# A first weight tile read in permuted row order, in two transfers, with x copied into the same order

## The chip, the core and the metric

The kernel runs on one core of a Trainium2 chip. The metric is the device time of one launch in microseconds (us). Three runs of the kernel before took 184.22, 182.49 and 182.88 us; the median is 182.88 us. One of them, the one of 184.22 us, was recorded by the hardware profiler, and every duration quoted below is from that execution.

## What is computed

For each of four batch entries the kernel takes a window of 64 consecutive rows of x, which starts at a row given at run time, and multiplies it by one shared matrix w:

```python
B, S, D, W = 4, 4096, 4096, 64
for b in range(B):
    o = int(offsets[b])
    results.append(x[b, o:o+W] @ w)      # x: B x S x D, w: D x D, float32
return np.stack(results)                 # 4 x 64 x 4096, float32
```

Together this is one product of 256 rows with a 4096 x 4096 matrix. w is 64 MiB in float32 and every element of it is read once; the four windows of x are 4 MiB, the output is 4 MiB.

## The kernel before

**Tiling.** The contracted dimension (4096) is cut into 32 k tiles of 128 rows of w. The 256 rows of x are two groups, g = 0 and 1, of 128. A product step is a matmul of a 128 x 128 piece of transposed x with a 128 x 512 piece of w, added up in a PSUM bank (`mm`, line 158).

**Loads of w.** Nearly all of w is loaded by the gpsimd (POOL) queue, which turns float32 into float16 on the way (`load_block`, line 84). The k tiles are loaded in blocks, `blocks` = (first tile, number of tiles): (0, 1), (1, 2), (3, 4), (7, 4), (11, 4), (15, 4), (19, 3), (22, 3), (25, 2), (27, 1). In a block of r tiles, partition p takes r consecutive rows of w, so that one contiguous run of DRAM fills it. `x_cols` picks the columns of x that belong to such an order of rows. Tiles 28 to 31 are loaded in six column pieces (line 122). The blocks go into a ring of three buffers (`wc_pool`, bufs=3): a load is issued only once the work that read the buffer's earlier content is done, and POOL waits for that in program order.

**The first k tile** is different. It is loaded without conversion by the sync (SP) queue, as float32, with one transfer whose pieces are 8 KB (half a row of w; line 67), into the first buffer of the same ring (`w0_32`, line 65). ScalarE (ACT) then converts it to float16 in two halves (line 70) into `w_one`. Row p of w lies on partition p.

**x.** The offsets come by the ACT queue (line 68). POOL loads each offset into a register and issues one transfer per batch entry (line 103), again converting, into `x16` (called `xrow` in the profile). These four transfers stand on the POOL queue behind block (1, 2) and ahead of block (3, 4). Then 64 matmuls with an identity transpose x (line 144), eight to a pair of PSUM banks; VectorE (DVE, line 153) and ACT (line 155) copy the pairs, in turn, to `xT`. All transposes stand ahead of the first product in PE's program order, and both conversions of line 70 stand ahead of line 155 in ACT's.

**Order of the work.** The schedule is written out by hand. `whole_rows(range(0, 3), True)` (line 190) multiplies k tiles 0, 1 and 2 for all columns, and DVE and ACT copy the sums to `acc` (lines 186 and 188). Then `whole_rows` runs once for each block from (3, 4) to (22, 3), and DVE adds the sums to `acc` (line 168). The last blocks and the tail pieces are done by column halves (`columns`, lines 206 to 217, and the loops behind it), and the results are stored from POOL, ACT and SP (line 204).

The three buffers of the ring are given out in this order: first tile, (1, 2), (3, 4), then (7, 4) in the first tile's buffer, (11, 4) in that of (1, 2), (15, 4) in that of (3, 4), and so on.

Of the kernel before, what the change touches and what calls it, by code (L numbers as in the profile page):

```python
# [10 lines left out]
def kernel(  # L11
# [7 lines left out]
    nc = tc.nc  # L19
    fp32 = mybir.dt.float32  # L20
    fp16 = mybir.dt.float16

    B, S, D = x.shape
    _, N = w.shape
    WIN = out.shape[1]
    P = 128
    NT = 512
    NG = N // 2
    n_k = D // P
    n_sub = NG // NT  # L30
    G = B // 2
# [7 lines left out]
    R_MAX = 4  # L39

    const_pool = ctx.enter_context(tc.tile_pool(name="const", bufs=1))
    x_pool = ctx.enter_context(tc.tile_pool(name="xp", bufs=1))
    wc_pool = ctx.enter_context(tc.tile_pool(name="wc", bufs=3))
# [6 lines left out]

    x16 = x_pool.tile([P, G * D], fp16, name="xrow")
    xT = [x_pool.tile([P, D], fp16, name=f"xT{g}") for g in range(G)]
    w_one = w1_pool.tile([P, N], fp16, name="w1")
    tmp = [acc_pool.tile([P, 2 * NT], fp32, name=f"tmp{i}") for i in range(G)]
    acc = [acc_pool.tile([P, N], fp32, name=f"acc{g}") for g in range(G)]
# [5 lines left out]

    ctx.enter_context(tc.manual_schedule())


    w0_32 = wc_pool.tile([P, R_MAX * N], fp16, name="wc", tag="wc")[:].bitcast(fp32)
    w0_32 = w0_32.rearrange("p (h n) -> p h n", h=2)[:, :, :NG]
    nc.sync.dma_start(out=w0_32, in_=w[0:P, :].rearrange("p (h n) -> p h n", h=2))
    nc.scalar.dma_start(out=off_t[:], in_=offsets[None, :])
    for h in range(2):
        nc.scalar.copy(out=w_one[:, h * NG : (h + 1) * NG], in_=w0_32[:, h, :])  # L70
    off_i32 = off_t.bitcast(mybir.dt.int32)


# [21 lines left out]
    for b in range(B):  # L95
# [8 lines left out]
            out=x16[b * PB : (b + 1) * PB, :],  # L104
            in_=x[b][bass.ds(o, WIN), :].rearrange("(p g) d -> p (g d)", g=G),
# [13 lines left out]
    for ng, st in zip(order, (steps, fine_steps)):  # L119
        for ki, n, c0, c1 in st:  # L120
            wd = c1 - c0
            nc.gpsimd.dma_start(  # L122
                out=t[:, pos : pos + n * wd].rearrange("p (t n) -> p t n", t=n),
                in_=w[ki * P : (ki + n) * P, ng * NG + c0 : ng * NG + c1].rearrange(
                    "(t p) n -> p t n", p=P
                ),
            )
            for q in range(n):
                for j in range(wd // NT):
                    a = pos + q * wd + j * NT  # L130
                    tail[(ki + q, (ng * NG + c0) // NT + j)] = t[:, a : a + NT]
            pos += n * wd

    def x_cols(g, kt):
        for k0, r in blocks:
            if k0 <= kt < k0 + r:
                a = k0 * P + kt - k0
                return x16[:, g * D + a : g * D + a + r * (P - 1) + 1 : r]
        return x16[:, g * D + kt * P : g * D + (kt + 1) * P]

    for g in range(G):
        for t in range(4):
            for i in range(8):
                nc.tensor.matmul(  # L144
                    out=pairs[t][:, i * P : (i + 1) * P],
                    lhsT=x_cols(g, 8 * t + i),
                    rhs=identity[:],
                    start=True,
                    stop=True,
                )  # L150
            dst = xT[g][:, 2 * t * NT : 2 * (t + 1) * NT]
            if t % 2 == 0:
                nc.vector.tensor_copy(out=dst, in_=pairs[t][:])  # L153
            else:
                nc.scalar.copy(out=dst, in_=pairs[t][:])  # L155
# [116 lines left out]
```

## Time and profile before

| | |
|---|---|
| median of three runs | 182.88 us (182.49 to 184.22) |
| the profiled execution: own time | 184.22 us |
| the profiled execution: span from first to last instruction | 182.4 us |
| TensorE (PE) busy | 128.3 us, 70% |
| DVE busy | 82.2 us, 45% |
| ACT busy | 16.8 us, 9% |
| queue q0 (POOL's), share of the 16 DMA engines | 92.2% |
| queue q1 (SP's), share of the 16 DMA engines | 4.6% |
| mean granted clock of TensorE | 0.926 |

The core has 16 DMA engines, and all queues run on them. The page's row "DMA" gives, in tenths, the mean busy share of these 16 in 40 equal slices of the span. A row of a queue gives its packets, their megabytes as written, and the time that they took as a share of 16 engines' span. Besides data a queue carries packets of 4 bytes, by which a DMA engine reports that its part of a transfer is done. In the tables of windows, "x" counts instructions, and the last three columns are PE's granted clock, the DMA share and GB/s.

### The profile page before, as it was taken

Reading aid. Unit: us, or ns where it says so; the run is one execution under the profiler, and the core shown is the slowest. Engines: PE = TensorE matmul, PEld = TensorE weight load, DVE = VectorE, ACT = ScalarE, POOL = GpSimd, SP = SyncE. Lnnn points to the kernel's source line nnn. Section 1 sums busy time; section 2 is a strip of 40 time slices with the busy share of each in tenths; the row PEclk is TensorE's granted clock in tenths of the full one; section 3 lists DMA queues with packets and bytes.
Section 4 is the critical chain, followed back from the end, with each engine's and each line's share of the span. In section 5 each row is a group of like instructions: output and inputs, shape, how many; then the busy total and the mean of one; then the engine's idle time right before and its main releaser. Section 6 shows DMA issues by size and latency. Waiting matters only on the chain.

```text
span 182.4 us, 1399 instructions
## 1 busy us (share of the span) xinstructions
PE 128.3 (70%) x576; PEld 57.5 (32%) x576; DVE 82.2 (45%) x68; ACT 16.8 (9%) x15; POOL 12.6 (7%) x27
## 2 busy tenths in 40 slices
PE   0000006998399929995899569999939999999920
PEld 0000006743134403442344224444403444444400
DVE  0000003845036722576077605779933893606570
ACT  2000802643000000000000000000000003104000
POOL 4400010001000010001000100011080000000200
PEclk9999999999969985999699978999975999999996
DMA  4999999999999799999999799999999999999696
GB/s 126 320 259 269 201 205 230 230 234 223 230 223 208 172 208 230 230 226 223 223 230 208 169 237 210 221 216 216 221 208 219 190 208 215 214 212 194 245 406 275
DMA packets 4007, 40.97 MB, mean 225 GB/s; under 512 B 418, under 2 KB 418, under 8 KB 2210
## 3 DMA queue, kind: packets, MB, share of 16 engines
q0 software_dynamic: 3152, 36.70, 92.2%
q1 hardware_dynamic: 560, 3.15, 4.6%
q10 hardware_dynamic: 290, 1.05, 1.4%
q8 instruction: 4, 0.07, 0.1%
q14 instruction: 1, 0.01, 0.0%
HBM read 71.30 MB, written 4.19 MB: 414 GB/s over the span
## 4 chain that ended last, share of the span: by engine, by line
DMA 62%; PE 26%; issue 4%; DVE 2%; POOLq 1%; DVEq 1%; POOL 1%
DMA wc<-in_w_dram 62%; PE banks L158 26%; DVE acc L168 2%; DVEq L267 1%; POOLq L96 1%; POOL xrow L103 0%; POOL identity masks.py:197 0%; POOLq L103 0%; POOL wc L84 0%; POOLq masks.py:199 0%; DVEq L168 0%; POOLq L256 0%
## 5 line engine op out<-in xcount | busy, mean ns | idle before, releaser
L158 PE MATMUL banks<-wc,xT 128*128 128x512 f16 x496 | 121.9, 405 | 17.2 <-DMA wc<-in_w_dram 17.0
L168 DVE TENSOR_TENSOR acc<-acc,banks 128x1024 f32<-128x1024 f32 x56 | 67.9, 1220 | 59.7 <-PE banks L158 58.7
L158 PEld LDWEIGHTS <-xT 128*128 128x128 f16 x512 | 52.3, 103 | 87.5 <-DMA wc<-in_w_dram 19.4
L144 PE MATMUL banks<-identity,xrow 128*128 128x128 f16 x64 | 5.4, 269 | 28.8 <-DMA xrow<-in_x_dram 28.8
L153 DVE CAST xT<-banks 128x1024 f16<-128x1024 f32 x4 | 4.8, 1222 | 30.5 <-PE banks L144 30.5
L213 ACT COPY tmp<-banks 128x1024 f32<-128x1024 f32 x4 | 3.9, 1016 | 118.5 <-PE banks L158 118.5
L144 PEld LDWEIGHTS <-xrow 128*128 128x128 f16 x64 | 5.3, 130 | 28.8 <-issue 28.8
L84 POOL DMA_DIRECT2D wc<-in_w_dram x9 | 4.9, 546 | 113.4 <-PE banks L158 96.9
L186 DVE COPY acc<-banks 128x1024 f32<-128x1024 f32 x4 | 4.9, 1225 | 4.5 <-PE banks L158 4.5
L158 PE MATMUL banks<-w,xT 128*128 128x512 f16 x16 | 6.1, 379 | 0.0
L70 ACT CAST w<-wc 128x2048 f16<-128x2048 f32 x2 | 3.7, 1894 | 16.3 <-DMA wc<-in_w_dram 16.3
L155 ACT CAST xT<-banks 128x1024 f16<-128x1024 f32 x4 | 3.9, 1014 | 8.7 <-PE banks L144 8.7
L217 DVE TENSOR_TENSOR acc<-acc,tmp 128x1024 f32<-128x1024 f32 x4 | 4.7, 1220 | 0.0
L188 ACT COPY acc<-banks 128x1024 f32<-128x1024 f32 x4 | 4.0, 1012 | 6.4 <-PE banks L158 6.4
L122 POOL DMA_DIRECT2D wc<-in_w_dram x6 | 3.9, 676 | 9.3 <-PE banks L158 9.3
L204 POOL DMA_DIRECT2D out_dram<-acc x2 | 1.1, 537 | 33.3 <-DVE acc L217 33.3
L103 POOL DMA_DIRECT2D xrow<-in_x_dram x4 | 2.0, 500 | 2.2 <-issue 2.2
L70 ACT ACT_TABLE_LOAD x1 | 1.3, 1283 | 1.4 <-PEq L256 1.4
masks.py:199 POOL TENSOR_SCALAR_AFFINE_SELECT identity<-identity 128x128 f16<-128x128 f16 x1 | 0.3, 287 | 0.1
masks.py:197 POOL MEMSET identity<- 128x128 f16 x1 | 0.2, 223 | 0.0
L256 POOL MEMSET const-float32-0.0<- 128x1 f32 x1 | 0.1, 98 | 0.4 <-issue 0.4
L256 POOL MEMSET const-bfloat16-1.0<- 128x1 bf16 x1 | 0.1, 102 | 0.0
(2 smaller groups left out, 0.2 us busy)
## 6 DMA issues: line engine op xcount, KB each, us to landing
wc<-in_w_dram POOLq DMA_DIRECT2D x4, 4096.0 KB, 42.0
wc<-in_w_dram POOLq DMA_DIRECT2D x2, 3072.0 KB, 34.3
wc<-in_w_dram POOLq DMA_DIRECT2D x2, 2048.0 KB, 20.2
wc<-in_w_dram POOLq DMA_DIRECT2D x4, 1024.0 KB, 26.7
wc<-in_w_dram SPq DMA_DIRECT2D x1, 2048.0 KB, 18.1
xrow<-in_x_dram POOLq DMA_DIRECT2D x4, 512.0 KB, 20.2
out_dram<-acc POOLq DMA_DIRECT2D x2, 1024.0 KB, 5.0
out_dram<-acc ACTq DMA_DIRECT2D x2, 512.0 KB, 4.5
```

The costliest lines, as they stand in the source:

```text
L70: nc.scalar.copy(out=w_one[:, h * NG : (h + 1) * NG], in_=w0_32[:, h, :])
L84: nc.gpsimd.dma_start(out=t[:, base : base + r * N], in_=w[k0 * P : (k0 + r) * P, :].rearrange("(p r) n -> p (r n)", r=r),)
L122: nc.gpsimd.dma_start(out=t[:, pos : pos + n * wd].rearrange("p (t n) -> p t n", t=n), in_=w[ki * P : (ki + n) * P, ng * NG + c0 : ng * NG ...
L144: nc.tensor.matmul(out=pairs[t][:, i * P : (i + 1) * P], lhsT=x_cols(g, 8 * t + i), rhs=identity[:], start=True, stop=True,)
L153: nc.vector.tensor_copy(out=dst, in_=pairs[t][:])
L155: nc.scalar.copy(out=dst, in_=pairs[t][:])
L158: nc.tensor.matmul(out=banks(bank), lhsT=xT[g][:, kt * P : (kt + 1) * P], rhs=rhs, start=start, stop=stop,)
L168: nc.vector.tensor_add(out=dst, in0=dst, in1=banks(bank, n))
L186: nc.vector.tensor_copy(out=dst, in_=banks(b0, 2))
L188: nc.scalar.copy(out=dst, in_=banks(b0, 2))
L213: nc.scalar.copy(out=tmp[g][:], in_=banks(4 * g + 2, 2))
L217: nc.vector.tensor_add(out=dst, in0=dst, in1=tmp[g][:])
```

## The change

The first k tile is loaded by two transfers on the sync queue, one for each half of the columns, in place of one. Partition 16 b + a now holds row 8 a + b of the tile, so neighbouring partitions lie 8 rows apart in DRAM; in the transfer's source the outermost dimension counts 8 (b), the next 16 (a), the last the 2048 columns. The tile is read into `acc[1]`, which is not otherwise used so early, in place of a buffer of the `wc` ring. The ring therefore gives its first buffer to block (1, 2), its second to (3, 4), its third to (7, 4), and its first again to (11, 4).

So that the products fit, the 128 columns of x that meet this tile are copied into the same order, into a new tile `x_first`, by two DVE copies (one for each g), ahead of the transposes. The transposes of k tile 0 read `x_first`; all others read `x16` as before.

```diff
+    x_first = x_pool.tile([P, G, P], fp16, name="xfirst")
...
-    w0_32 = wc_pool.tile([P, R_MAX * N], fp16, name="wc", tag="wc")[:].bitcast(fp32)
-    w0_32 = w0_32.rearrange("p (h n) -> p h n", h=2)[:, :, :NG]
-    nc.sync.dma_start(out=w0_32, in_=w[0:P, :].rearrange("p (h n) -> p h n", h=2))
+    w0_32 = acc[1]
+
+    w0_rows = w[0:P, :].rearrange("(a b) n -> b a n", b=8)
+    nc.sync.dma_start(out=w0_32[:, :NG], in_=w0_rows[:, :, :NG])
     nc.scalar.dma_start(out=off_t[:], in_=offsets[None, :])
-    for h in range(2):
-        nc.scalar.copy(out=w_one[:, h * NG : (h + 1) * NG], in_=w0_32[:, h, :])
+    nc.sync.dma_start(out=w0_32[:, NG:], in_=w0_rows[:, :, NG:])
+    nc.scalar.copy(out=w_one[:, :NG], in_=w0_32[:, :NG])
+    nc.scalar.copy(out=w_one[:, NG:], in_=w0_32[:, NG:])
...
     def x_cols(g, kt):
+        if kt == 0:
+            return x_first[:, g, :]
...
+    for g in range(G):
+        nc.vector.tensor_copy(
+            out=x_first[:, g, :].rearrange("p (b a) -> p b a", b=8),
+            in_=x16[:, g * D : g * D + P].rearrange("p (a b) -> p b a", b=8),
+        )
```

## Prediction

> **What bounds the kernel now.** I read the page's row of the DMA engines first, then its list of queues, then PE in order of time.
>
> ```profile
> DMA  4999999999999799999999799999999999999696
> q0 software_dynamic: 3152, 36.70, 92.2%
> q1 hardware_dynamic: 560, 3.15, 4.6%
> q10 hardware_dynamic: 290, 1.05, 1.4%
> ```
>
> The 16 DMA engines are busy from the second slice to the last loads; three queues take 98% of their time. The question for any edit is therefore what it does to the work of a DMA engine. PE shows how they pass it on:
>
> ```profile
> 48.71 15.67 PE L158 MATMUL banks<-wc,xT 128*128 128x512 f16 x64 [3.93 <-DMA wc<-in_w_dram]
> 68.02 16.64 PE L158 MATMUL banks<-wc,xT 128*128 128x512 f16 x64 [3.63 <-DMA wc<-in_w_dram]
> 87.29 15.55 PE L158 MATMUL banks<-wc,xT 128*128 128x512 f16 x64 [2.63 <-DMA wc<-in_w_dram]
> 106.61 26.03 PE L158 MATMUL banks<-wc,xT 128*128 128x512 f16 x112 [3.77 <-DMA wc<-in_w_dram]
> 135.66 4.88 PE L158 MATMUL banks<-wc,xT 128*128 128x512 f16 x11 [3.02 <-DMA wc<-in_w_dram]
> ```
>
> Landings start the blocks, 19.3 us apart for four tiles, and PE needs some 16 us for one. The last wait ends at 135.66; from there PE works almost without a break to 174.4, and the last adds and stores follow. If block (22, 3) and the loads behind it land later by d, the end comes later by d.
>
> In the trace's DMA records a transfer ends with one 4-byte report from each DMA engine that took part. Every load of POOL has 16, close together: those of (22, 3) lie between 133.8 and 135.3 us. A packet of a four-tile block takes 2.43 us, eight per engine make 19.45 us, the step of the landings: each engine runs through its own list without a gap, and a block has landed when the **slowest** engine is through.
>
> **The change part by part.**
>
> *The spread of the first tile.* Before, it is 256 packets of 8 KB; an undisturbed one takes 309 ns. q1's 560 packets are these 256, 256 of the stores and 48 reports: three transfers over 16 engines each. So each engine carried 16 of the tile's packets, 16 x 0.309 = 4.94 us. q10 shows another spread: its 290 are 256 of the stores, 32 reports, and for the offsets one packet with **one** report. A transfer with 128 rows outermost went over 16 engines, one with a single row over one. The new source has 8 outermost, between these rows. Its least cost is 0, if it still uses 16 engines. The other end is one engine, 256 x 0.309 = 79 us; I exclude it, since a single row leaves nothing to share out and eight groups do. I take eight engines, one per group, as an estimate from the two rows. Then each of eight engines carries 32 packets, 9.9 us, and the others none: the heavy eight gain 16 x 0.309 = **4.94 us** of work, and the light eight have none of this tile.
>
> [...]
>
> *What can be won back.* Blocks are dealt out in equal parts, so the light engines can't help, and the heavy ones never run dry: 4.94 us stays with them to the last load. If the engines that report latest (135.1 to 135.3, three of 16) were all among the light ones, the end would move up to 1.5 us less; for three at random that is one chance in ten (8/16 x 7/15 x 6/14), so I take off nothing. On the other side, the 256 packets took 92.8 us as recorded, 363 ns in the mean with slow ones at the start; 16 x 0.363 = 5.8 us, 0.9 more.
>
> *Rows 8 apart.* The pieces stay 8 KB. The nearest rows are the tail loads of 4 KB packets, which read pieces of 8 KB that lie 16 KB apart at 0.324 us each: at most 16 x 0.015 = 0.2 us more, at least 0. I take 0.
>
> *The second issue on SP* takes about 0.63 us, as the first at 0.87, and is over before the first data packet at 2.30 us. Behind it SP only has stores, after a wait of 173.1 us. 0. ACT's issue of the offsets does not move.
>
> *The start: ACT behind the second half.* In order of time, before:
>
> ```profile
> 19.02 3.70 ACT L70 CAST w<-wc 128x2048 f16<-128x2048 f32 x2 [16.33 <-DMA wc<-in_w_dram]
> 23.01 0.53 POOL L84 DMA_DIRECT2D wc<-in_w_dram  x1 [15.64 <-ACT w L70]
> 28.84 5.44 PE L144 MATMUL banks<-identity,xrow 128*128 128x128 f16 x64 [28.84 <-DMA xrow<-in_x_dram]
> 30.75 1.01 ACT L155 CAST xT<-banks 128x1024 f16<-128x1024 f32 x1 [8.03 <-PE banks L144]
> ```
>
> The tile has the engines to itself from 2.3 to 6.0 us; nine packets per engine go through. Then q0's packets alternate with it, one for one: seven more packets, the last beside block (1, 2). On a heavy engine 23 packets are left at 6.0. Block (1, 2) and x are 16 packets of 1.227 us with 16 to 20 of the tile's 0.322 between them: x lands at 6.0 + 19.6 + 5.2 to 6.4, about 31 to 32.5 us on the slowest engine in place of 28.4. The four to nine turns left alternate with packets of 2.43 us, 2.75 us a turn, so the **second half lands between 42 and 56 us**. ACT's conversion of it (1.9 us) stands ahead of all copies of line 155, and without them PE cannot finish the transposes. The first products, at 34.26 before, then start at 47 to 61, and end 10.5 us later at 57 to 71, in place of 44.8. Behind them POOL waits to issue (11, 4), at 45.08 before. But q0 still holds (7, 4): the heavy engines have work until 67.6 + 4.9 = 72.5, the light ones until about 65. PE then runs four-tile blocks in 14 to 16 us against 19.45, and is waiting for loads again after one to three blocks. So this delay of 12 to 26 us costs **0 at the end**, as long as (11, 4) reaches the heavy engines by 72.5; the light ones have some 7 us in hand, the heavy ones' 4.9 and the 7 x 0.322 = 2.3 that they no longer carry behind 6.0.
>
> *Two copies to x_first.* No such DVE row exists; the nearest is line 153, 1.22 us for 1024 columns. An eighth of it is 0.15 us, so a copy costs 0.15 to 1.22; I take 0.2. The first transposes wait for one, and line 153 stands behind both. All of it lies in the same cover, and without it 0.4 us would come on the path.
>
> *The buffer.* POOL's wait of 15.64 us ahead of (7, 4) goes; its issue moves from 23.01 to about 7.4. Its data can't move before (3, 4) is through at 48.3, so this wins 0; the next wait is that for (11, 4), just priced. acc[1]'s first other writers follow products that need both conversions anyway: 0.
>
> *PE's clock.* After the wait at 135.66 the granted clock is 0.50 from 136 to 140 and 0.79 to 144, 5.7 us at half speed, some 2.8 us of work. A shifted wait can meet it otherwise; half of this either way, 1.4 us, is an estimate; I take 0.
>
> The sum is +4.9 us. The profiled execution took 184.22 (span 182.4, 1.8 around it) and would take 189.1, with a span of 187.3. It was the slowest of three, 1.34 above the median; the median becomes 182.88 + 4.9 = **187.8**.
>
> **The rivals.**
>
> *Still 16 engines.* The permuted source is spread like any 128 rows. For it speaks that the destination still has 128 rows; against it, the offsets' single report. Then the load per engine is unchanged, the copies are hidden, and it takes 182.9: not slower.
>
> *The heavy engines run dry.* With the first products ending at 71, the issue of (11, 4), and 1.8 to 4.6 us to its first packet (POOL's first load: issued at 1.38, first packet at 5.99), it comes at up to 75.6, 3.1 us after 72.5: 187.8 + 3.1 = 190.9. It decides once the first products end later than about 68 us. Against it stands that this is the late end of every step.
>
> *Faster.* Sixteen engines, and the last wait shifted so that the clock's 5.7 us at half speed go: 182.9 - 2.8 = 180.1. For it speaks only that the mean clock differs from block to block; against it, that the change moves no landing then.
>
> **How the numbers follow.** Eight engines without a gap 0.83; 16 engines 0.09; heavy engines dry 0.05; faster 0.03. The first case spans 187.8 - 2.0 (late engines and clock, mostly one or the other) to 187.8 + 2.3 (slow packets and clock), 185.8 to 190.1. That holds about 0.95 x 0.83 = 0.79; with a little of the third case 190.4 reaches 0.8. Changes within 1% are about what a measurement of this kernel can't tell from none. Slower by over 1%: 0.83 + 0.05; within 1%: 0.09; faster 0.03.
>
> **What would show it.** q1's packets: 256 + 256 + 32 reports of stores + 2 x 8 = 560 with eight engines, 576 with sixteen. x landing near 32 and the first products ending at 57 to 71, not 45; the reports of a block in two groups some 7 us apart; PE's last wait ending near 140.6. The prediction is wrong if the second group isn't there, if the heavy engines have a gap after 65 us, or if the last PE wait is set by something other than a load.

## The result, and the profile after

The change makes the kernel **20 us slower**: 202.92 us (202.54 to 204.88) against 182.97 us (182.49 to 184.41), six runs each, a ratio of 1.109 (95% interval 1.103 to 1.116). The direction was forecast, the size was not: the prediction was 187.8 us, its range ended at 190.4. The profiled execution has a span of 201.0 us, 18.6 more than the one before.

The page's row of the DMA engines and its queues, of the kernel after:

```profile
DMA  4999999999999859999999998999999999985697
q0 software_dynamic: 3152, 36.70, 87.3%
q1 hardware_dynamic: 560, 3.15, 6.9%
```

q1 has the 560 packets that eight engines leave; the trace's DMA records show 8 reports for each of the two transfers. But the queue's share rose from 4.6% of 182.4 us to 6.9% of 201.0, with the same bytes: its packets became slow. The same 256 pieces took 92.8 us together before and 173.7 after, 679 ns in the mean.

PE in order of time, the waits for a landing and the work ahead of them:

```profile
73.32 28.39 PE L167 MATMUL banks<-wc,xT 128*128 128x512 f16 x130
107.04 16.15 PE L167 MATMUL banks<-wc,xT 128*128 128x512 f16 x64 [5.33 <-DMA wc<-in_w_dram]
126.37 13.99 PE L167 MATMUL banks<-wc,xT 128*128 128x512 f16 x64 [3.18 <-DMA wc<-in_w_dram]
140.88 10.53 PE L167 MATMUL banks<-wc,xT 128*128 128x512 f16 x48 [0.53 <-DMA wc<-in_w_dram]
155.49 37.46 PE L167 MATMUL banks<-wc,xT 128*128 128x512 f16 x160 [4.08 <-DMA wc<-in_w_dram]
```

The last wait ends at 155.49 in place of 135.66, 19.8 us later; behind it PE's path is 1.2 us shorter. So all of the loss lies ahead of this wait. Where, is told by the landings at the start (time of issue and time to landing, from the lists of DMA issues) and by PE's waits:

| us | (1, 2) landed | x landed | (3, 4) landed | PE's wait for (11, 4) | for (22, 3) |
|---|---|---|---|---|---|
| before | 19.2 | 28.8 | 48.7 | 87.29 | 135.66 |
| after | 27.8 | 48.7 | 68.3 | 107.04 | 155.49 |
| later by | 8.6 | 19.9 | 19.6 | 19.8 | 19.8 |

The lists of DMA issues give size and time from issue to landing; block (1, 2) is issued at 1.38 us in both, the last transfer of x at 6.34 and block (3, 4) just behind it. Before, then after:

```profile
wc<-in_w_dram POOLq DMA_DIRECT2D x1, 2048.0 KB, 17.8
xrow<-in_x_dram POOLq DMA_DIRECT2D x1, 512.0 KB, 22.4
wc<-in_w_dram POOLq DMA_DIRECT2D x1, 4096.0 KB, 41.8
```

```profile
wc<-in_w_dram POOLq DMA_DIRECT2D x1, 2048.0 KB, 26.5
xrow<-in_x_dram POOLq DMA_DIRECT2D x1, 512.0 KB, 42.3
wc<-in_w_dram POOLq DMA_DIRECT2D x1, 4096.0 KB, 61.5
```

8.6 us are lost up to block (1, 2), 11.3 more up to the last transfer of x, and nothing from there on. The reports of (7, 4) show the two sets of engines: eight between 69.8 and 70.5 us, eight between 85.9 and 87.3. Below, the early and the late engines are these two sets; a piece is an 8 KB packet of the first tile. The windows up to block (1, 2) and up to x, before and then after, show engines that are busy and move little:

```profile
2.30:19.20 16.90, 0.00 (x0) 0.00 (x0) 0.00 (x0) 0.57 (x2) 2.83 (x6) 1.00 1.04 271
19.20:28.80 9.60, 0.00 (x0) 0.00 (x0) 0.00 (x0) 3.52 (x2) 0.53 (x1) 1.00 1.09 232
```

```profile
2.30:27.80 25.50, 0.00 (x0) 0.00 (x0) 0.00 (x0) 1.65 (x2) 3.36 (x7) 1.00 1.05 185
27.80:48.70 20.90, 0.00 (x0) 0.00 (x0) 0.00 (x0) 0.64 (x1) 0.00 (x0) 1.00 1.02 178
```

The busy share (next to last column) is about 1 throughout, and the GB/s (last) fall from 271 and 232 to 185 and 178: not waiting for work, but slow packets. Between 4 and 10 us the tile's pieces took 681 to 946 ns instead of 309 to 399, between 18 and 48 us 516 to 1394, and POOL's packets of 1.226 us up to 2.56.

### The profile page after: what moved, and what is told of

It is laid out like the page before. It is cut to its first block, busy times and chain, and to the rows that moved or that the text cites. A ratio compares the mean times of both kernels' runs of the same rounds, so it can differ in the third digit from the quotient of the medians.

```text
span 201.0 us, 1408 instructions
## 1 busy us (share of the span) xinstructions
PE 123.5 (61%) x576; PEld 57.4 (29%) x576; DVE 82.7 (41%) x70; ACT 16.8 (8%) x15; POOL 12.6 (6%) x27
## 3 DMA queue, kind: packets, MB, share of 16 engines
q0 software_dynamic: 3152, 36.70, 87.3%
## 4 chain that ended last, share of the span: by engine, by line
DMA 47%; issue 32%; PE 15%; DVE 2%; DVEq 1%; POOL 0%; POOLq 0%
DMA wc<-in_w_dram 47%; PE banks L167 15%; DVE acc L177 2%; DVEq L276 1%; POOL wc L86 0%; POOLq L86 0%; DVEq L177 0%; POOLq L265 0%
## 5 line engine op out<-in xcount | busy, mean ns | idle before, releaser
L167 PE MATMUL banks<-wc,xT 128*128 128x512 f16 x496 | 115.2, 389 | 13.4 <-DMA wc<-in_w_dram 13.1
L167 PEld LDWEIGHTS <-xT 128*128 128x128 f16 x512 | 50.7, 100 | 78.7 <-DMA wc<-in_w_dram 15.6
L153 PE MATMUL banks<-identity,xfirst 128*128 128x128 f16 x2 | 0.6, 299 | 49.1 <-DVE xfirst L146 49.1
L146 DVE COPY xfirst<-xrow 128x128 f16<-128x128 f16 x2 | 0.5, 268 | 48.8 <-DMA xrow<-in_x_dram 48.8
L153 PE MATMUL banks<-identity,xrow 128*128 128x128 f16 x62 | 7.0, 310 | 7.0 <-ACT xT L164 7.0
L153 PEld LDWEIGHTS <-xrow 128*128 128x128 f16 x62 | 6.6, 147 | 7.2 <-issue 7.2
L72 ACT CAST w<-acc 128x2048 f16<-128x2048 f32 x1 | 1.9, 1897 | 29.3 <-DMA acc<-in_w_dram 29.3
L71 ACT CAST w<-acc 128x2048 f16<-128x2048 f32 x1 | 1.9, 1897 | 23.8 <-DMA acc<-in_w_dram 23.8
```

The lines of the kernel that those rows point to most:

```text
L71: nc.scalar.copy(out=w_one[:, :NG], in_=w0_32[:, :NG])
L153: nc.tensor.matmul(out=pairs[t][:, i * P : (i + 1) * P], lhsT=x_cols(g, 8 * t + i), rhs=identity[:], start=True, stop=True,)
L167: nc.tensor.matmul(out=banks(bank), lhsT=xT[g][:, kt * P : (kt + 1) * P], rhs=rhs, start=start, stop=stop,)
```

## The experiments

Theories at the outset. **DRAM**: rows that lie 8 apart are read slowly. **SBUF**: the eight engines, each with 16 neighbouring partitions to write, slow each other down. **Eight engines**: a transfer on few engines is slow as such.

### The first tile alone, in six orders (m1)

```diff
+    sources = [
+        w[0:P, half],                                                            # A
+        w[0:P, :].rearrange("(a b) n -> b a n", b=8)[:, :, half],                # B, the change
+        w[0 : 2 * P, :].rearrange("(b c a) n -> c b a n", c=2, a=16)[0][:, :, half],  # C
+        w[0:P, :].rearrange("(a b) n -> b a n", b=16)[:, :, half],               # D
+        w[0 : 9 * 16, :].rearrange("(a c) n -> c a n", c=9)[:8][:, :, half],     # E
+        w[0 : 8 * P, :].rearrange("(p c) n -> c p n", c=8)[0][:, half],          # F
+    ]
+    for src in sources:
+        nc.sync.dma_start(out=acc[0][:, half], in_=src)
+        nc.vector.tensor_copy(out=acc[1][:, half], in_=acc[0][:, half])
```

> Only transfers of one half tile (128 pieces of 8 KB) on SP's queue, each after the one before has landed, with nothing else on the DMA engines; no product is computed, the output is not that of the reference. In order: A natural rows; B the change's (8 groups, rows 8 apart); C 8 groups of 16 adjacent rows; D 16 groups, rows 16 apart; E 8 groups, rows 9 apart; F 128 rows, each 8 after the one before, not grouped; G natural rows, other half. Theory DRAM (the order of the rows in DRAM makes the pieces slow): B, D and F have pieces of 600 to 900 ns, A, C, E and G of 309. Theory SBUF (eight engines that each write 16 neighbouring partitions get in each other's way): B, C and E have 600 to 900 ns, A, F and G 309, D 309 to 600. If it takes POOL's packets beside it: all have 309 ns, and B, C and E take 5 us, the others 2.5.

| | groups and rows | reports | median piece, ns | first to last packet, us |
|---|---|---|---|---|
| A | natural | 16 | 309 | 3.9 |
| B | 8 groups, 8 apart | 8 | 616 | 9.3 |
| C | 8 groups, adjacent | 8 | 606 | 9.2 |
| D | 16 groups, 16 apart | 16 | 569 | 4.7 |
| E | 8 groups, 9 apart | 8 | 579 | 9.3 |
| F and G | 128 rows 8 apart; natural | 16 | 309 | 5.9 for both |

DVE copies each half once it has landed; its waits for A to E show the same (they hold the issue and the report as well):

```profile
5.98 1.23 DVE L40 COPY acc<-acc 128x2048 f32<-128x2048 f32 x1 [5.98 <-DMA acc<-in_w_dram]
19.08 1.23 DVE L40 COPY acc<-acc 128x2048 f32<-128x2048 f32 x1 [11.87 <-DMA acc<-in_w_dram]
31.77 1.23 DVE L40 COPY acc<-acc 128x2048 f32<-128x2048 f32 x1 [11.46 <-DMA acc<-in_w_dram]
40.07 1.23 DVE L40 COPY acc<-acc 128x2048 f32<-128x2048 f32 x1 [7.07 <-DMA acc<-in_w_dram]
53.05 1.23 DVE L40 COPY acc<-acc 128x2048 f32<-128x2048 f32 x1 [11.75 <-DMA acc<-in_w_dram]
```

The order in DRAM does nothing: rows 8 apart are as fast as natural ones without groups (F), and adjacent rows as slow as the change's with groups (C). Here pieces take nearly double in every order with groups outermost (579 to 616 ns against 309), with 16 reports too (D, 569); m2 below shows for which groups this holds. DRAM falls; D speaks against eight engines. With nothing beside them the change's pieces take twice their time (616 ns, B); I had taken 309 ns for granted.

### Undoing the permutation, doing it with 16 groups, keeping the groups without it (u1, u2, u3)

```diff
 u1: two transfers, no x_first
-    w0_rows = w[0:P, :].rearrange("(a b) n -> b a n", b=8)
+    # the two transfers read w[0:P, :NG] and w[0:P, NG:]
 u2:
-    "(a b) n -> b a n", b=8
+    "(a b) n -> b a n", b=16
 u3:
-    w0_rows = w[0:P, :].rearrange("(a b) n -> b a n", b=8)
+    w0_rows = w[0 : 2 * P, :].rearrange("(b c a) n -> c b a n", c=2, a=16)[0]
```

> The change without its permutation: two transfers of half rows into acc[1], rows in natural order, x not copied. Both theories: 16 engines, q1 with 576 packets, x at 28 us, 183 us (181.5 to 184.5). If the two transfers, acc[1] or the freed buffer carry the loss: 195 to 203.

> The change with 16 groups in place of 8: partition 8 b + a holds row 16 a + b, so rows lie 16 apart and the outermost count is 16. q1 with 576 packets. Theory DRAM: the pieces take 600 ns or more, spread over 16 engines: 188 to 195. Theory SBUF: each engine writes 8 neighbouring partitions, 183 to 188.

> The change with 8 groups whose 16 rows are adjacent in DRAM (the groups 32 rows apart), partitions and copies as in the change; the rows are not those that belong to the first tile, so the product of this tile is another. q1 with 560 packets. Theory DRAM: pieces of 309 ns, the eight engines 4.9 us late, 186 to 189.5. Theory SBUF: as the change, 200 to 206.

| | us | ratio to before (95%) | pieces, mean ns | (3, 4), last report |
|---|---|---|---|---|
| u1 | 182.22 | 0.997 (0.995 to 0.999) | 351 | 47.6 |
| u2 | 184.22 | 1.007 (1.005 to 1.009) | 445 | 49.7 |
| u3 | 203.80 | 1.112 (1.107 to 1.117) | 695 | 67.7 |

Line of q1 on the pages of u1, u2 and u3, in this order:

```profile
q1 hardware_dynamic: 576, 3.15, 4.6%
```

```profile
q1 hardware_dynamic: 576, 3.15, 5.4%
```

```profile
q1 hardware_dynamic: 560, 3.15, 6.9%
```

u3 repeats the change to its landings with rows that are adjacent, so neither DRAM nor the exact rows matter. u1 acquits the two transfers, acc[1] and the freed buffer; it is even 0.6 us faster than before. Of this 0.4 us is its first packet, which leaves at 1.88 us instead of 2.30 (SP's first issue takes 0.38 us instead of 0.63); the rest was not looked for. In u2 each engine carries 16 pieces of 445 ns, 7.1 us, against 5.8 before: 1.3 more; block (3, 4) is through 1.4 later than before (48.3) and the kernel takes 1.4 more. There the copies to x_first are included and cost nothing at the end.

### Which partitions meet (m2)

```diff
+    for groups, each in [(8, 16), (8, 8), (8, 4), (8, 2), (2, 32), (2, 16), (2, 64), (2, 2)]:
+        src = w[0:n, :].rearrange("(a b) n -> b a n", b=groups)    # n = groups * each
+        # four transfers of half rows into acc[0] and more, then one DVE add of both
```

> Only transfers of 8 KB pieces on SP's queue, four to a pattern, each pattern after the one before has landed, nothing else on the DMA engines; no product is computed, the output is not that of the reference. A pattern is (groups x partitions in a group): 8x16, 8x8, 8x4, 8x2, 2x32, 2x16, 2x64, 2x2, all with rows as many apart as there are groups. [...] Theory eight engines (few engines or permuted rows are slow as such): all patterns of 8 have about 600 ns, whatever their groups. Theory neighbours (an engine that writes many neighbouring partitions is slow): slower with more partitions in a group, 2x64 the slowest.

| groups x partitions | 8x16 | 8x8 | 8x4 | 8x2 | 2x32 | 2x16 | 2x64 | 2x2 |
|---|---|---|---|---|---|---|---|---|
| median piece, ns | 604 | 447 | 309 | 606 | 309 | 309 | 309 | 633 |
| mean | 551 | 470 | 336 | 530 | 360 | 323 | 314 | 544 |

The patterns differ in the number of their groups and in how far apart these begin. Eight groups of four take 309 ns, so eight engines as such are not slow; many neighbours in a group aren't either (2x64, 309). Groups of two, whose neighbours begin 2 partitions apart, take twice as long (606 ns in 8x2, 633 in 2x2). 2x32 has a median of 309. In its order of time it starts slow, with pieces of 629 and 627, after two quick pairs 639 to 652; bit by bit this fades, and by 17 us into it most pieces take 309 again. 8x8 has values all the way from 309 to some 620. In 8x16, the change's groups, neighbouring groups begin 16 partitions apart, as in 2x16, where a piece takes 309; the pieces of 8x16 stay near 600 through all 35 us. In 8x16, 8x8 and 2x32 some groups begin 32 partitions apart, in 8x4, 2x16 and 2x64, all at 309, none. So groups 32 apart are the likely cause in the change; this is a reading of these times, no record names the partition or the engine of a piece. Why 2x32 gets back to 309 and 8x16 doesn't is open.

### Eight engines kept apart (v1)

```diff
+    def load_first(c0, c1):
+        for p in range(0, P, 32):
+            rows = w[p : p + 32, :].rearrange("(a b) n -> b a n", b=8)
+            nc.sync.dma_start(out=w0_32[p : p + 32, c0:c1], in_=rows[:, :, c0:c1])
```

> The change with the first tile in eight transfers of 32 partitions, each of 8 groups of 4 (rows 8 apart, x copied to match): still eight engines with 32 pieces each, but each writes four partitions of its own. q1 with 256 + 256 + 64 + 32 = 608 packets. Theory SBUF: pieces of 309 to 322 ns, x at 31 to 33 us, (3, 4) landed at 52 to 54, the last wait of PE at 140 to 141.5, 186.5 to 189.5 us. Theory eight engines: as the change, 198 to 204.

209.87 us, 1.147 of before (1.144 to 1.151): slower than the change, the opposite of what I expected, and at first sight a verdict against SBUF. Two things overlap here. The pieces did get better: 309 to 322 ns up to 15 us and again from 35 us on, 496 in the mean against 679; the last report of (3, 4) came at 57.3, not 68.0, and that of (7, 4) at 78.3, not 87.3. But between 15 and 36 us, when x's transfers move, 80 of 88 took 519 to 1175 ns even in groups of four. And the end was set by something else. POOL in v1:

```profile
6.83 1.09 POOL L90 DMA_DIRECT2D wc<-in_w_dram  x2
90.96 0.54 POOL L90 DMA_DIRECT2D wc<-in_w_dram  x1 [83.04 <-PE banks L171]
```

Eight transfers have eight reports per engine instead of two, each takes a turn beside POOL's packets (four pieces beside packets of 2.43 us make 4 x 2.75 = 11.0 us; from one transfer's reports to the next, at 35.5 and 48.9 us, it was 13.4, one packet of 2.43 more), and the second half landed only at 73.4 us. ACT's conversion came late, and with it the first products and the issue of (11, 4), at 90.96. The engines were through with (7, 4) at 78.3, the early ones at 65.5: **all 16 stood dry**, and (11, 4) was through on all of them between 112.1 and 113.6. This is the prediction's rival of dry engines, in an experiment instead of in the change. In the change the issue came at 74.22, 13 us ahead of the late engines' 87.3.

### The spread by itself (w1, w2, w3)

The tile is moved out of the start, so that it neither meets x nor holds up the first products:

```diff
+    w0_32 = x16[:].bitcast(fp32)        # after the transposes
 w1:
+    nc.sync.dma_start(out=w0_32, in_=w[0:P, :])
 w2:
+    for p in range(0, P, 32):
+        rows = w[p : p + 32, :].rearrange("(a b) n -> b a n", b=8)
+        nc.sync.dma_start(out=w0_32[p : p + 32, :], in_=rows)
 w3:
+    nc.sync.dma_start(out=w0_32, in_=w[0:P, :].rearrange("(a b) n -> b a n", b=8))
...
-    whole_rows(range(0, 3), True)
+    whole_rows(range(1, 3), True)
+        # tile 0 is converted and multiplied with block (15, 4)
```

> The first tile is taken out of the start: one transfer of whole rows (natural order, 16 KB pieces, 16 engines) into the x buffer once the transposes have read it, converted and multiplied together with block (15, 4). It meets none of x's transfers, and no product waits for it. The base for the next two. Same work on each engine as before, starting some 1.5 us later: 182 to 185.5 us.

> As w1, but in four transfers of 32 partitions, 8 groups of 4, on eight engines (x copied to match): the uneven spread alone. Every theory that holds the 4.94 us of the spread right: w1 + 4.9 (4 to 6), pieces of 16 KB at 618 to 640 ns. If uneven lists cost more by themselves: w1 + 10 or more.

> As w1, but in one transfer of 8 groups of 16 partitions, as the change has them. Theory SBUF (engines meet at the ways into neighbouring partitions): more than w2, by up to 16 x 0.62 = 9.9 us if all pieces meet another engine, by little if the pieces rarely meet, as they are on the engine a fifth of the time beside POOL's packets of 2.43 us. If meeting x's transfers was what cost most in the change: w2 + 0 to 3.

| | us | ratio to before (95%) | pieces, mean ns | per engine | (22, 3), last report |
|---|---|---|---|---|---|
| w1 | 183.05 | 1.001 (0.999 to 1.003) | 622 | 5.0 us | 135.8 |
| w2 | 189.17 | 1.034 (1.032 to 1.037) | 667 | 10.7 us | 141.0 |
| w3 | 192.22 | 1.053 (1.049 to 1.057) | 772 | 12.4 us | 143.3 |

w2 against w1 is close to the predicted 4.94 us: 5.7 more engine time, (22, 3) 5.2 later, 6.1 us at the end, just above the 4 to 6 expected. The groups cost 2.3 us more on the landing (w3 against w2), 3.1 at the end. So beside POOL's packets of blocks of w groups cost a little (772 ns a piece against 667); why so little, no run shows. It is not the 15 us that the change lost beyond the spread.

### Even engines beside x (x1)

```diff
+    nc.vector.tensor_copy(out=w0_32[:, 0:N:NG], in_=t[:, 0 : 2 * N : N])   # waits for block (1, 2)
+    nc.sync.dma_start(out=w0_32[:, :NG], in_=w[0:P, :NG])
+    nc.sync.dma_start(out=w0_32[:, NG:], in_=w[0:P, NG:])
```

> Two transfers of half rows in natural order on 16 engines, as in u1, but issued once block (1, 2) has landed (a small copy from that block ahead of them), so that they move beside x's four transfers of 32 partitions each. Theory meeting x: pieces of 600 to 1000 ns and POOL's 16 KB packets above 1.3 us while x moves, (3, 4) landed 2 to 6 us later than in u1, 184 to 188 us. If only the change's eight groups are disturbed: pieces of 322 ns, (3, 4) landed within 1 us of u1, 182 to 184.

The times spread from 187.24 to 191.96 us, so there is no verdict on them; the packets are plain. Beside x the pieces took 322 to 616 ns, POOL's 16 KB packets 1.226 us as ever, and (3, 4) was through at 48.3 us, 0.7 behind u1. On sixteen engines plain rows lose next to nothing beside x. What these runs lose against the 182 to 184 expected is again late products: in the profiled execution (191.29 us) the second half landed at 55.5 us and (11, 4) was issued at 72.44, behind the end of (7, 4) at 68.9; between 69 and 73 us next to no data moved.

### x moved behind block (3, 4) (y1, y2)

```diff
 both, on the change and on u1:
     load_block(*blocks[1])
+    load_block(*blocks[2])
     ... x's four transfers ...
-    for k0, r in blocks[2:]:
+    for k0, r in blocks[3:]:
```

> The change with POOL's transfers of x moved behind block (3, 4), so that the first tile's pieces beside blocks (1, 2) and (3, 4) meet no transfer of x; x and the first products come later. Theory x (the eight groups lose most where they meet x's transfers, which write 32 partitions at a time): 8 KB pieces beside block (3, 4) mostly at 322 to 620 ns, and 700 to 1200 only once x moves; the eight late engines 8 to 13 us behind those of y2. Theory groups (eight groups of 16 partitions are this slow early in any company): pieces of 700 to 1200 ns beside (3, 4) too, 15 to 20 us behind y2.

> The base for y1: u1 (two half transfers, plain rows, 16 engines) with x's transfers behind block (3, 4). Same engine work as u1; the first products end at about 64 us, just ahead of the end of what is queued, so 182 to 186 us.

y1 took 203.66 us (1.112 of before, 1.105 to 1.119), y2 184.26 (1.008, 1.005 to 1.011). In y1 block (1, 2) landed at 23.1 us, (3, 4) at 49.8 and x at 66.7, 5.1, 12.4 and 19.4 behind y2. By this y1 is nearer to "groups". The packets say more (medians from the DMA records of y1, ns, over stretches of 2 us in the first row and of 5 us in the third):

| us | what moves | tile's pieces | POOL's packets |
|---|---|---|---|
| 4 to 10 | the tile, (1, 2) on the early engines | 719 to 932 | 1229 to 1568 |
| 12 to 30 | (1, 2) and (3, 4) | 322 | 1226, 2432 |
| 35 to 60 | x: first on the early engines, beside (3, 4) on the late ones | 580 to 999 | 1273 to 1954; 2448 to 3901 |
| 60 to 65 | x on the late engines, (7, 4) on the early ones, no tile | | 2039; 2901, up to 4100 |

So the groups lose at the very start, where the tile is nearly alone, and again as soon as the early engines come to x, at about 35 us; between the two, beside packets of 1226 and 2432 ns that write blocks of w, hardly anything is slow (322 ns). And in the last row x's packets take 2.04 us with no piece of the tile left. About 1 us of y1's end is late products: (11, 4) was issued at 83.84, and the late engines were through with (7, 4) at 84.7.

### x written over all partitions (z1, z2)

```diff
 both, on the change and on u1:
-            out=x16[b * PB : (b + 1) * PB, :],
-            in_=x[b][bass.ds(o, WIN), :].rearrange("(p g) d -> p (g d)", g=G),
+            out=x16[:, b * NG : (b + 1) * NG],
+            in_=x[b][bass.ds(o, WIN), :].rearrange("r (h d) -> (r h) d", h=2),
```

> The change with each transfer of x written over all 128 partitions (half rows of x, 8 packets of 4 KB per engine at 0.324 us, 2.6 us, in place of 2 of 1.226) instead of 32; the bytes are the same, but x lies in other places, so the products are of other rows and columns. Theory narrow x (the loss beyond the spread arises where x's 32 partitions are written while the engines are out of step): pieces beside x mostly 322 to 620 ns, x landed within 7 us of z2, the late engines 4 to 8 us behind z2, 187 to 192 us. If any transfers beside the eight groups lose as much: x 15 us or more behind z2, 198 to 204 us.

> The base for z1: u1 (two half transfers, plain rows, 16 engines) with x's transfers written over 128 partitions in the same way; the products are of other rows and columns of x. Per engine 32 x 0.324 = 10.4 us for x in place of 9.8: u1 + 0.6, 182.3 to 184.

z1 took 198.78 us (1.086 of before, 1.085 to 1.088), z2 182.36 (0.996, 0.995 to 0.998). The narrow form of x is a part of the loss, not the whole: (3, 4) lands 14.7 us behind z2 (62.6 against 47.9), against 19.6 for the change, and x's last reports come 15.3 us behind z2 (42.9 against 27.6). The theory "narrow x" falls as the main cause. What remains in z1 is all pieces: 637 ns in the mean, 20.4 us per late engine against 5.7 in z2, a difference of 14.7, just the delay. Beside packets of 0.324 us its pieces took 600 to 800 ns from 21 us on, about what B's took in m1 with nothing beside them (616 ns) or more; beside packets of 1.226 and 2.432 us, in y1, they took 322. Why short packets beside them leave the pieces slow and long ones don't is not shown.

### The sum over the runs

Engine time of the tile's pieces on a late engine (in u2 on any), less that of its base, against the delay of a landing behind the tile:

| run, base | pieces, us per engine | more than the base | last report of | later by |
|---|---|---|---|---|
| u2, before | 7.1 | 1.3 | (3, 4) | 1.4 |
| w2, w1 | 10.7 | 5.7 | (22, 3) | 5.2 |
| w3, w1 | 12.4 | 7.4 | (22, 3) | 7.5 |
| v1, before | 15.9 | 10.1 | (7, 4) | 10.7 |
| z1, z2 | 20.4 | 14.7 | (7, 4) | 14.6 |
| y1, y2 | 18.1 | 12.5 | (7, 4) | 17.9 |
| the change, before | 21.7 | 15.9 | (7, 4) | 19.7 |

In the first five rows the pieces explain the delay to within 0.6 us. Where the eight groups meet x in its narrow form (y1 and the change), 4 to 5 us come on top: POOL's own packets became slower. Its packets of 16 and 32 KB took 115 us more in the change than before, on all 16 engines together. But they took 60 us more in v1 too, and recorded times overlap a little (the DMA shares above read 1.02 to 1.09), so the match to 0.6 us is closer than the method can promise.

## Why the prediction was right, and where it was wrong

- **What bounds the kernel, and that a delay of the loads reaches the end one for one.** Right: 19.8 us at the last wait, 20.0 us in the median.
- **The spread over eight engines.** Right: 560 packets, 8 reports per transfer. Its price was 4.94 us; w2 against w1 has 5.2 at (22, 3) and 6.1 at the end. Eight engines, one per group, was an estimate from two rows; m1 shows it for a count of eight (8 reports in B, C and E, 16 in D). Which eight engines these are, no run shows. The rival of 16 engines is out.
- **The step that failed is the price of a piece**: 32 pieces of 0.309 us on a heavy engine, with "at most 16 x 0.015 = 0.2 us more, at least 0. I take 0" for the rows 8 apart, and 0.9 us for slow pieces. (All 32 pieces are read 8 rows apart, so that bound should have been 0.5 us; it changes nothing here.) A piece took 679 ns in the mean. I had asked only for the DRAM side of the new order. That side costs nothing (F, u3); the loss is on the other side, where the transfer is cut into eight shares of 16 neighbouring partitions: 604 ns a piece for 8x16 in m2, with nothing else moving, against 309 for eight shares of four (8x4). On a late engine the pieces came to 21.7 us in place of the 9.9 predicted. Less the 5.8 of before that is 15.9 of the 19.7; POOL's packets, which I had left as they were, bring the rest. How much of the pieces' loss beside x comes from the groups and how much from x itself is not shown: v1's pieces, in groups of four like those of 8x4 at 309 ns, also came to 15.9 us per late engine.
- **"What can be won back": nothing.** Right; the early eight reported 16.8 us ahead at (7, 4), and this helped no one. The two groups were to be 7 us apart.
- **The start.** Right in kind, late in time: x landed at 48.7 (31 to 32.5 predicted), the second half at 57.7 (42 to 56), (11, 4) was issued at 74.22. ACT's conversion of the second half stood ahead of line 155's copies, as the trace after shows:

```profile
57.75 1.90 ACT L72 CAST w<-acc 128x2048 f16<-128x2048 f32 x1 [29.31 <-DMA acc<-in_w_dram]
59.55 1.92 ACT L164 CAST xT<-banks 128x1024 f16<-128x1024 f32 x2
```

- **That this late start costs nothing at the end.** Right in the change, but with luck: the condition was that (11, 4) reaches the heavy engines by 72.5 us, and it was issued only at 74.22. It still came in time because the same slow pieces held these engines until 87.3. PE's waits for (11, 4) and (15, 4) are 19.3 us apart as before. POOL's issues after:

```profile
74.22 0.54 POOL L86 DMA_DIRECT2D wc<-in_w_dram  x1 [66.31 <-PE banks L167]
88.03 0.53 POOL L86 DMA_DIRECT2D wc<-in_w_dram  x1 [13.28 <-PE banks L167]
```

  The early engines did stand idle, from 70.5 to the first packets of (11, 4) at 75.6 us. The limit was rightly named as well: v1 crosses it.
- **The copies to x_first.** 0.27 us each against 0.2 taken, hidden:

```profile
L146 DVE COPY xfirst<-xrow 128x128 f16<-128x128 f16 x2 | 0.5, 268 | 48.8 <-DMA xrow<-in_x_dram 48.8
```

- **The freed buffer and the second issue on SP.** Nothing, as said (u1, 0.6 us faster than before).
- **PE's clock.** Taken as 0; behind the last wait PE's path was 1.2 us shorter (its matmuls took 37.46 us at a granted clock of 0.95, before 38.73 at 0.92), within the 1.4 allowed.

Not settled: what slows a given piece in the change, and why the pieces of v1, whose groups of four took 309 ns alone in m2, take up to 1.17 us beside x. That the late engines' x collides with the early engines' next block, in the 32 partitions that x writes, is argued from y1's packets at 60 to 65 us (2.04 us) and x1's undisturbed ones (1.226); no run isolates it.

## What to carry to other kernels

Where DMA engines bound a kernel, ask of every new access pattern how many engines it is cut over and which partitions one engine then writes: the trace answers the first with the number of reports, and the price of the second shows in the time of one packet, not in its bytes. A reordering of DRAM rows cost nothing here (309 ns in F); the outermost count of eight that came with it doubled the time of a piece (616 ns in B) and put the pieces on half of the engines (8 reports for 16). And a late first product is free only as long as the loads already queued last: (11, 4) issued at 74 us cost nothing, at 91 it set the end.

## What the runs showed of the hardware

- With nothing else moving, pieces of 8 KB took 606 and 633 ns in the median in groups of two partitions (8x2, 2x2), 604 in eight groups of 16 (8x16), and 309 in 8x4, 2x16 and 2x64 (m2). 2x32 began at 627 to 652 ns and within 17 us was mostly at 309 again; 8x16 stayed near 600 for 35 us.
- x's packets, which write 32 partitions at a time, took 1.226 us with 16 engines and plain rows, beside pieces of the tile too (x1), and about 2.04 us once half of the engines were ahead on another block (y1, 60 to 65 us). That the uneven engines are the cause is argued, not isolated.
- The first of two transfers of half rows was issued faster than one transfer with two pieces per row (0.38 against 0.63 us, u1), and its data started 0.42 us earlier. u1 is the only version here faster than before with the same output, by 0.3%.
